# RMSNorm with relu: the scale and relu of eight rows in one vector instruction

## The chip, the cores and the metric

The kernel runs on one core of a Trainium2 chip. The metric is the device time of one execution in microseconds (us).

VectorE is called DVE in the profile, ScalarE is ACT, and SP is SyncE, which issues the large DMAs. "The period" below is the time from the start of one group of 8 rows on VectorE to the start of the next.

## The reference

```
x: 16 x 1024 x 512 float32, gamma: 512 float32, eps: 1e-5
rms    = sqrt(mean(x ** 2, over the last axis) + eps)
x_norm = x / rms * gamma
return maximum(x_norm, 0)
```

It reads 33.5 MB and writes 33.5 MB, and does little arithmetic on each element.

## The kernel before

The 16384 rows are cut into 8 chunks. A chunk has 16 rows on each of 128 partitions (4 MB) and lives in one of six slots. Everything is done in place in the slot. A chunk is computed in two groups of 8 rows (G = 8), so there are 16 groups in all.

```
K = 16
G = 8
nchunks = rows // K          # 8
nslots = 6
ngroups = K // G             # 2
# ... cut: pools, tiles, load() and store() of a whole chunk from SP ...

def compute(i):
    xt = slot[i % nslots]
    for g in range(ngroups):
        a, b = g * G, (g + 1) * G
        for j in range(a, b):
            nc.scalar.activation(out=junk, in_=xt[:, j, :], func=ACTF.Square,
                                 accum_out=ss[i][:, j:j + 1])
        nc.scalar.activation(out=rms[i][:, a:b], in_=ss[i][:, a:b],
                             func=ACTF.Sqrt, bias=eps_sb, scale=inv_d)
        nc.vector.tensor_mul(out=xt[:, a:b, :], in0=xt[:, a:b, :], in1=gammaG())
        nc.vector.reciprocal(out=rstd[i][:, a:b], in_=rms[i][:, a:b])
        for j in range(a, b):
            nc.vector.tensor_scalar(
                out=xt[:, j, :], in0=xt[:, j, :],
                scalar1=rstd[i][:, j:j + 1], scalar2=0.0,
                op0=ALU.mult, op1=ALU.max)

# ... cut: gamma copied to all partitions ...
for i in range(min(nslots, nchunks)):
    load(i)
for i in range(min(nslots, nchunks)):
    compute(i)
nxt = nslots
for i in range(nchunks):
    store(i)
    if i >= 1 and nxt < nchunks:
        load(nxt)
        compute(nxt)
        nxt += 1
```

`gammaG()` is gamma with a step of 0 over the eight rows: the same 512 values are read again for each row, with an innermost step of 1.

## Time and profile before

| | before |
|---|---|
| time, median | 164.25 us (163.35 to 164.48; 164.11 when the prediction was made) |
| span of the profile | 162.0 us |
| VectorE busy | 124.6 us, 77% |
| ScalarE busy | 98.5 us, 61% |
| large DMA queue, share of 16 engines | 96.9% |

These are lines of the page of the kernel before: busy time by engine, the 40 slices of VectorE and DMA (a digit is the busy share of a slice in tenths), the queue with the share of all 16 engines' time, the chain of waits that ended last (shares of the span by engine), and the two costliest vector groups (busy time in all, mean ns of one, then idle time before it).

```profile
DVE 124.6 (77%) x164; ACT 98.5 (61%) x274; POOL 0.2 (0%) x4
...
DVE  1001299999999999999999999999999999920000
...
DMA  6999899999999999998999999999999999999990
...
q1 hardware_dynamic: 2304, 67.11, 96.9%
...
DVE 74%; DMA 8%; ACT 3%; issue 2%; DVEq 0%
...
L78 DVE TENSOR_TENSOR slot<-slot,gamma_sb 128x4096 f32<-128x4096 f32 x16 | 70.7, 4418 | 4.2 <-ACT junk L74 4.2
L81 DVE TENSOR_SCALAR slot<-slot,rstd 128x512 f32<-128x512 f32 x128 | 52.1, 481 | 0.6
```

The averages (77%, 97%) leave open which engine sets the time, and the chain of waits (74% VectorE) seems to name VectorE. The slices say more. VectorE works without a gap from slice 6 to slice 35 and does nothing in the last four; from its end at 142.99 us to the end of the span it is idle for 19 us, while DMA is full until nearly the end.

The next lines are the timeline of VectorE for one period (start in us, duration in us, what). A mean of 481 ns for one tensor_scalar includes its overlap with the next (eight times 481 ns would be 3.85 us, and the eight below take 3.26 from the first start to the last end).

```profile
57.78 4.42 DVE L78 TENSOR_TENSOR slot<-slot,gamma_sb 128x4096 f32<-128x4096 f32 x1
62.12 0.19 DVE L79 RECIPROCAL rstd<-rms 128x8 f32<-128x8 f32 x1
62.35 3.26 DVE L81 TENSOR_SCALAR slot<-slot,rstd 128x512 f32<-128x512 f32 x8
65.52 4.42 DVE L78 TENSOR_TENSOR slot<-slot,gamma_sb 128x4096 f32<-128x4096 f32 x1
```

From start to start the multiply by gamma takes 4.34 us, the reciprocal 0.23 and the eight tensor_scalars 65.52 - 62.35 = 3.17. The period is 7.74 us. The multiply spends 1.06 ns on an element of a partition, the tensor_scalars 3.17 / 4096 = 0.77 ns with their fixed costs included.

The last store is issued when VectorE is done. Below are SP's own waits (waiter, what it waited for, us in total, times, longest); the second line is the wait for the last store. After them stand two stretches of the windows view: stretch and length, busy time of DVE, ACT and POOL, granted clock, DMA share, GB/s.

```profile
SPq L62 <- DVE slot L81: 94.5, 7, 20.7
...
SPq L133 <- DMA out_dram<-slot: 17.6, 1, 17.6
```

```profile
155.00:158.00 3.00, 0.00 (x0) 0.00 (x0) 0.00 (x0) 1.00 0.94 404
158.00:161.00 3.00, 0.00 (x0) 0.00 (x0) 0.00 (x0) 1.00 0.05 22
```

The last store of 4 MB needs 17.6 us after its issue, though 4 MB take 9.8 us at 430 GB/s, the rate of the windows view from 92 to 110 us. It stands in line behind earlier stores: DMA is near full up to 158 us, and the windows from 143 to 158 us (426 GB/s for 7 us, 446 for 5, 404 for 3) come to 6.4 MB, 2.2 MB more than the last store has.

### The profile page before, as it was taken

Reading aid. Unit: us, or ns where it says so; the run is one execution under the profiler, and the core shown is the slowest. Engines: PE = TensorE matmul, PEld = TensorE weight load, DVE = VectorE, ACT = ScalarE, POOL = GpSimd, SP = SyncE. Lnnn points to the kernel's source line nnn. Section 1 sums busy time; section 2 is a strip of 40 time slices with the busy share of each in tenths; the row PEclk is TensorE's granted clock in tenths of the full one; section 3 lists DMA queues with packets and bytes.
Section 4 is the critical chain, followed back from the end, with each engine's and each line's share of the span. In section 5 each row is a group of like instructions: output and inputs, shape, how many; then the busy total and the mean of one; then the engine's idle time right before and its main releaser. Section 6 shows DMA issues by size and latency. Waiting matters only on the chain.

```text
span 162.0 us, 554 instructions
## 1 busy us (share of the span) xinstructions
DVE 124.6 (77%) x164; ACT 98.5 (61%) x274; POOL 0.2 (0%) x4
## 2 busy tenths in 40 slices
DVE  1001299999999999999999999999999999920000
ACT  2107999999999999999999199901998000000000
POOL 0000000000000000000000000000000000000000
DMA  6999899999999999998999999999999999999990
GB/s 227 421 405 502 388 413 493 390 421 477 396 421 471 396 388 388 461 445 388 463 437 404 453 445 404 453 437 396 461 429 445 429 421 445 429 421 445 437 413 16
DMA packets 2315, 67.14 MB, mean 414 GB/s; under 512 B 260, under 2 KB 260, under 8 KB 264
## 3 DMA queue, kind: packets, MB, share of 16 engines
q1 hardware_dynamic: 2304, 67.11, 96.9%
q14 instruction: 3, 0.02, 0.0%
q10 hardware_dynamic: 8, 0.01, 0.0%
HBM read 33.56 MB, written 33.55 MB: 414 GB/s over the span
## 4 chain that ended last, share of the span: by engine, by line
DVE 74%; DMA 8%; ACT 3%; issue 2%; DVEq 0%
DVE slot L78 43%; DVE slot L81 30%; DMA slot<-in_x_dram 8%; ACT junk L74 3%; DVE rstd L79 1%; DVEq L133 0%
## 5 line engine op out<-in xcount | busy, mean ns | idle before, releaser
L74 ACT ACTIVATE junk<-slot 128x512 f32<-128x512 f32 x128 | 76.8, 600 | 23.0 <-DMA slot<-in_x_dram 19.5
L78 DVE TENSOR_TENSOR slot<-slot,gamma_sb 128x4096 f32<-128x4096 f32 x16 | 70.7, 4418 | 4.2 <-ACT junk L74 4.2
L81 DVE TENSOR_SCALAR slot<-slot,rstd 128x512 f32<-128x512 f32 x128 | 52.1, 481 | 0.6
L74 ACT ACTIVATION_READ_ACCUMULATOR junk<-slot 128x1 f32 x128 | 23.8, 186 | 0.0
L93 DVE LOAD_MASK_SELECT gamma_sb<-gseed x1 | 0.0, 14 | 12.8 <-DMA gseed<-in_gamma_dram 12.8
L76 ACT ACTIVATE rms<-ss,eps_sb 128x8 f32<-128x8 f32 x16 | 4.8, 301 | 0.5
L74 ACT ACT_TABLE_LOAD x1 | 1.3, 1283 | 3.2 <-issue 3.2
L79 DVE RECIPROCAL rstd<-rms 128x8 f32<-128x8 f32 x16 | 3.1, 194 | 0.0
L76 ACT ACT_TABLE_LOAD x1 | 1.3, 1283 | 0.0
L86 DVE MEMSET gseed<- 128x512 f32 x1 | 0.5, 485 | 0.9 <-PEq L119 0.9
L93 DVE STREAM_SHUFFLE gamma_sb<-gseed 128x512 f32<-128x512 f32 x1 | 0.7, 721 | 0.0
L119 POOL MEMSET const-bfloat16-1.0<- 128x1 bf16 x1 | 0.1, 101 | 0.0
L119 POOL MEMSET const-uint8-127<- 128x1 uint8 x1 | 0.1, 101 | 0.0
L119 POOL MEMSET const-float32-0.0<- 128x1 f32 x1 | 0.1, 99 | 0.2 <-issue 0.2
L119 POOL MEMSET const-float32-1.0<- 128x1 f32 x1 | 0.1, 98 | 0.0
L87 DVE MEMSET eps_sb<- 128x1 f32 x1 | 0.1, 59 | 0.0
## 6 DMA issues: line engine op xcount, KB each, us to landing
slot<-in_x_dram SPq DMA_DIRECT2D x8, 4096.0 KB, 30.6
out_dram<-slot SPq DMA_DIRECT2D x8, 4096.0 KB, 35.4
gseed<-in_gamma_dram ACTq DMA_DIRECT2D x4, 2.0 KB
```

The source lines that it names most:

```text
L74: nc.scalar.activation(out=junk, in_=xt[:, j, :], func=ACTF.Square, accum_out=ss[i][:, j:j + 1])
L76: nc.scalar.activation(out=rms[i][:, a:b], in_=ss[i][:, a:b], func=ACTF.Sqrt, bias=eps_sb, scale=inv_d)
L78: nc.vector.tensor_mul(out=xt[:, a:b, :], in0=xt[:, a:b, :], in1=gammaG())
L79: nc.vector.reciprocal(out=rstd[i][:, a:b], in_=rms[i][:, a:b])
L81: nc.vector.tensor_scalar(out=xt[:, j, :], in0=xt[:, j, :], scalar1=rstd[i][:, j:j + 1], scalar2=0.0, op0=ALU.mult, op1=ALU.max)
L86: nc.vector.memset(gseed, 0.0)
L87: nc.vector.memset(eps_sb, eps)
L93: nc.vector.stream_shuffle(gamma_sb, gseed, [0] * 32)
L119: nc = _bacc.Bacc("TRN2", target_bir_lowering=False, num_devices=1)
```

## The change

The intent is fewer vector instructions: eight small tensor_scalars per group become one scalar_tensor_tensor over all eight rows. It takes the max with 0 first and then multiplies by the row factor, which gives the same because the factor is positive. The row factor comes in as a second tensor, with a step of 0 along the row.

```diff
             nc.vector.reciprocal(out=rstd[i][:, a:b], in_=rms[i][:, a:b])
-            for j in range(a, b):
-                nc.vector.tensor_scalar(
-                    out=xt[:, j, :], in0=xt[:, j, :],
-                    scalar1=rstd[i][:, j:j + 1], scalar2=0.0,
-                    op0=ALU.mult, op1=ALU.max)
+            r = rstd[i][:, a:b]
+            rb = bass.AP(tensor=r.tensor, offset=r.offset,
+                         ap=[r.ap[0], r.ap[1], [0, d]])
+            nc.vector.scalar_tensor_tensor(
+                out=xt[:, a:b, :], in0=xt[:, a:b, :], scalar=0.0, in1=rb,
+                op0=ALU.max, op1=ALU.mult)
```

## The prediction

What is cut out of the recorded text is marked: figures and reasons for the rate of vector instructions, for their fixed cost and for a penalty on the step of 0 that no trace of this case showed. No cut figure is a term of the forecast's sum: 160.8 + 12.2 + 1.1 us comes to a span of 174, and with 2.1 us to a time of 176 us.

> # Prediction
>
> **What bounds the kernel now.** The page: span 162.0 us, VectorE (DVE) busy 77%, ScalarE 61%, DMA queue 96.9%. Two resources are nearly full. The chain that ended last runs 74% through VectorE; in the timeline its work is gapless from 19.09 us to 142.99 us, 16 groups at a period of 7.74 us, and the waits show none for it after 19.09. The last 4 MB store is issued at 143.0 and lands about 160.9, 17.6 us later, although 4 MB at 430 GB/s takes 9.8 us: the windows show DMA at 0.94 or more until 158 us, so that store stands behind a backlog of about 6 us. That backlog is all the slack that VectorE has.
>
> **What the change does.** Per group of 8 rows it removes 8 tensor_scalars (128x512) and adds one scalar_tensor_tensor over 128x4096, whose row factor is read with an innermost step of 0. 128 vector instructions become 16; order, loads, stores and ScalarE work stay.
>
> Removed: eight tensor_scalars take 3.26 us together, 0.407 us for 512 elements. [...] the multiply by gamma (two tensors, 128x4096) takes 4.42 us, cadence 4.33.
> Added: the new instruction has two tensor operands[...]; estimated from that multiply, 4.42 us, cadence 4.33. The saved fixed costs (7 per group[...]) are already inside the 3.26. So +1.1 us per group, period 8.8 to 8.9 us: +17 to +18 us of vector time (124.6 to about 142).
>
> **On the critical path.** VectorE ends at 19.1 + 16 x 8.85 = about 160.7 us instead of 143.0. Chunks are ready every 17.7 us while the remaining stores need 9.8 each, so the queue is empty when the last store is issued (some microseconds of DMA idle before the last two stores). It then takes about 12 us (the first load, unqueued, took 12.3) instead of 17.6: 5.5 us are hidden. Span 160.8 + 12.2 + 1.1 = 174; time is span + 2.1: **176 us**, +7%. Range 172 to 181. Faster by over 2%: 0.02; within 2%: 0.03; slower by over 2%: 0.95.
>
> **What would show each step.** scalar_tensor_tensor x16 at about 4.4 us (right)[...]. DVE busy about 142 us, gapless to about 160.7, no new wait. DMA share about 90%, low slices before the last store. SP's wait for the last store about 12 us. ScalarE busy unchanged.
>
> **What would make it wrong.** The read with innermost step 0 of a 4-byte operand. [...] I give any such penalty 10%. If the last store still finds a backlog, add 2 to 4 us; if it lands in 10.5 us, take 1.5 off.

## The result, and the profile after

| | before | after |
|---|---|---|
| time, median | 164.25 us | 175.74 us (175.59 to 175.76) |
| ratio to before | | 1.0708 (95% interval 1.0673 to 1.0743) |
| span | 162.0 us | 173.8 us |
| VectorE busy | 124.6 us | 143.3 us |
| vector instructions | 164 | 52 |
| VectorE ends at | 142.99 us | 161.64 us |
| wait for the last store | 17.6 us | 10.7 us |

A ratio is the mean time of one kernel's fast runs over that of the other's fast runs of the same rounds, so it is not quite the ratio of the medians.

The lines of the page after that answer to those of before:

```profile
DVE 143.3 (82%) x52; ACT 98.5 (57%) x274; POOL 0.2 (0%) x4
...
DVE  1001699999999999999999999999999999999100
...
DMA  6999899999999999989999999998989808930885
...
q1 hardware_dynamic: 2304, 67.11, 90.3%
...
DVE 49%; ACT 23%; issue 14%; DMA 7%
...
L78 DVE TENSOR_TENSOR slot<-slot,gamma_sb 128x4096 f32<-128x4096 f32 x16 | 70.7, 4419 | 4.1 <-ACT junk L74 4.1
L83 DVE SCALAR_TENSOR_TENSOR slot<-slot,rstd 128x4096 f32<-128x4096 f32 x16 | 70.8, 4425 | 0.5
```

The new instruction takes 4425 ns, the same as the multiply by gamma beside it. VectorE has a third of its former instructions and 18.7 us more of busy time. DMA has gaps (0, 3 and 0 tenths) in the last eight slices; before, only the very last slice was empty.

The chain of waits gives VectorE only 49% now, although VectorE does more. This share must not be read as relief. In the chain of this run, five of the last twelve new instructions are booked as "issue" in pieces of 4.31 us, and the first 54 us are traced back through ScalarE. The timeline shows VectorE without a wait from 19.03 us to its end. One period of it, after:

```profile
59.00 0.19 DVE L79 RECIPROCAL rstd<-rms 128x8 f32<-128x8 f32 x1
59.23 4.42 DVE L83 SCALAR_TENSOR_TENSOR slot<-slot,rstd 128x4096 f32<-128x4096 f32 x1
63.58 4.42 DVE L78 TENSOR_TENSOR slot<-slot,gamma_sb 128x4096 f32<-128x4096 f32 x1
67.91 0.20 DVE L79 RECIPROCAL rstd<-rms 128x8 f32<-128x8 f32 x1
68.14 4.42 DVE L83 SCALAR_TENSOR_TENSOR slot<-slot,rstd 128x4096 f32<-128x4096 f32 x1
```

From start to start the new instruction takes 4.35 us where the eight took 3.17, and the period is 68.14 - 59.23 = 8.91 us. The difference of 1.17 us comes 16 times, 18.7 us in all. The time rose by 11.5 us. The remaining 7 us are in the wait for the last store and in the windows at the end of the run:

```profile
SPq L62 <- DVE slot L83: 117.2, 7, 23.1
...
SPq L134 <- DMA out_dram<-slot: 10.7, 1, 10.7
```

```profile
155.00:158.00 3.00, 2.97 (x3) 0.00 (x0) 0.00 (x0) 1.00 0.00 0
158.00:161.00 3.00, 3.00 (x1) 0.00 (x0) 0.00 (x0) 1.00 0.00 0
161.00:165.00 4.00, 0.64 (x1) 0.00 (x0) 0.00 (x0) 1.00 0.75 319
```

DMA is idle from 155 to 161 us while VectorE works on the last group. The last store finds the queue empty and takes 10.7 us, 6.9 less than before.

### The profile page after: what moved, and what is told of

Its sections match the earlier page's. It is cut to its first block, busy times and chain, and to the rows that moved or that the text cites. A ratio compares the mean times of both kernels' runs of the same rounds, so it can differ in the third digit from the quotient of the medians.

```text
span 173.8 us, 415 instructions
## 1 busy us (share of the span) xinstructions
DVE 143.3 (82%) x52; ACT 98.5 (57%) x274; POOL 0.2 (0%) x4
## 3 DMA queue, kind: packets, MB, share of 16 engines
q1 hardware_dynamic: 2304, 67.11, 90.3%
## 4 chain that ended last, share of the span: by engine, by line
DVE 49%; ACT 23%; issue 14%; DMA 7%
DVE slot L78 30%; ACT junk L74 21%; DVE slot L83 18%; DMA slot<-in_x_dram 7%; ACT rms L76 1%; DVE rstd L79 1%; ACT L76 1%
## 5 line engine op out<-in xcount | busy, mean ns | idle before, releaser
L83 DVE SCALAR_TENSOR_TENSOR slot<-slot,rstd 128x4096 f32<-128x4096 f32 x16 | 70.8, 4425 | 0.5
```

The lines of the kernel that those rows point to most:

```text
L83: nc.vector.scalar_tensor_tensor(out=xt[:, a:b, :], in0=xt[:, a:b, :], scalar=0.0, in1=rb, op0=ALU.max, op1=ALU.mult)
```

## The experiments

There are two claims to test. The first is about the instruction: with the second tensor the rate is halved, and that costs more than the saved instructions give; the step of 0 has no part in it. The second is about the critical path: DMA is a floor, VectorE's work is free up to a certain end, and then each microsecond counts. The rivals were that long instructions are slow as such, that the step of 0 costs, and that VectorE's work counts in proportion. Twelve kernels ran. Each ratio is to the kernel before in the same rounds.

### e1_ts_one: one tensor_scalar over eight rows

```diff
-            for j in range(a, b):
-                nc.vector.tensor_scalar(
-                    out=xt[:, j, :], in0=xt[:, j, :],
-                    scalar1=rstd[i][:, j:j + 1], scalar2=0.0,
-                    op0=ALU.mult, op1=ALU.max)
+            nc.vector.tensor_scalar(
+                out=xt[:, a:b, :], in0=xt[:, a:b, :],
+                scalar1=rstd[i][:, a:a + 1], scalar2=0.0,
+                op0=ALU.mult, op1=ALU.max)
```

> Wrong result on purpose: the kernel before with ONE tensor_scalar over 128x4096 per group (row factor of the group's first row for all 8 rows). Only the count changes, from 8 to 1; the operation keeps its single tensor source. Theory (element rate decides, count only adds a fixed cost of about 0.13 us each):[...] about 2.27 us per instruction against 3.17 us for the eight; period about 6.8 us. Rival 1 ([...] the length is the culprit): about 4.4 us. For the time: theory of DMA as the floor says 164, same as before, although VectorE loses about 14 us of work; rival 2 (VectorE's work counts one for one, as its 74% of the chain suggests) says about 150.

The fixed cost of 0.13 us is measured at e12.

Measured: 163.98 us, ratio 0.9987 (0.9963 to 1.0011). The timeline of VectorE:

```profile
60.63 4.42 DVE L78 TENSOR_TENSOR slot<-slot,gamma_sb 128x4096 f32<-128x4096 f32 x1
64.96 0.19 DVE L79 RECIPROCAL rstd<-rms 128x8 f32<-128x8 f32 x1
65.19 2.35 DVE L80 TENSOR_SCALAR slot<-slot,rstd 128x4096 f32<-128x4096 f32 x1
67.46 4.42 DVE L78 TENSOR_TENSOR slot<-slot,gamma_sb 128x4096 f32<-128x4096 f32 x1
```

From start to start the tensor_scalar takes 67.46 - 65.19 = 2.27 us, as expected, and the multiply by gamma of the same size 64.96 - 60.63 = 4.33. So a long tensor_scalar keeps its rate (0.55 ns per element with the fixed cost, where the eight short ones have 0.77 and the multiply 1.06), and merging eight into one would save 0.90 us per group if the operation could stay what it is. It can't: one tensor_scalar has one factor per partition, and the eight rows need eight (the result of e1 was wrong by a relative error of 0.041). The time did not move although VectorE lost 14.3 us of busy time (110.3 against 124.6): the rival by which each vector microsecond counts is out. VectorE ended at 132.4 us, 10.6 us earlier than before (not 14.3, because it waited 3.7 us more for ScalarE), and SP waited for the last store 10.6 us longer, 28.2 in place of 17.6:

```profile
SPq L132 <- DMA out_dram<-slot: 28.2, 1, 28.2
```

### e2_stt_eight: the new operation, still eight times

```diff
+            for j in range(a, b):
+                r = rstd[i][:, j:j + 1]
+                rb = bass.AP(tensor=r.tensor, offset=r.offset,
+                             ap=[r.ap[0], [0, d]])
+                nc.vector.scalar_tensor_tensor(
+                    out=xt[:, j, :], in0=xt[:, j, :], scalar=0.0, in1=rb,
+                    op0=ALU.max, op1=ALU.mult)
```

(in place of the one instruction over eight rows)

> Right result: the changed kernel with its instruction cut into eight, scalar_tensor_tensor on 128x512 with the row factor read at step 0, so the kind of instruction changes and the count of 8 stays. Theory:[...] 0.60 to 0.66 us each, 4.8 to 5.3 us per group, period 9.4 to 9.9 us, VectorE ends at 170 to 177 us, time 184 to 191. So fewer instructions did help, by 0.5 to 1 us per group, and the rate lost more. Rival (the count is worth nothing when the rate is the same): 4.35 us per group and 176.

Measured: 183.61 us, ratio 1.1184 (1.1168 to 1.1201).

```profile
61.17 4.90 DVE L84 SCALAR_TENSOR_TENSOR slot<-slot,rstd 128x512 f32<-128x512 f32 x8
66.00 4.42 DVE L78 TENSOR_TENSOR slot<-slot,gamma_sb 128x4096 f32<-128x4096 f32 x1
```

VectorE ended at 169.3 us. End and time lie just under the expected ranges (170 to 177 and 184 to 191), because the instructions came out at the low edge of theirs, 0.604 us each. From start to start the eight take 4.83 us, so the count is worth something (0.48 us per group against 4.35 for one), and the rival that gives it no worth is out. Four corners are now known, in us per group from start to start:

| | eight of 128x512 | one of 128x4096 |
|---|---|---|
| tensor_scalar, one tensor source | 3.17 (before) | 2.27 (e1) |
| scalar_tensor_tensor, two tensor sources | 4.83 (e2) | 4.35 (after) |

Going right gains 0.9 or 0.5 us. Going down loses 1.7 or 2.1. The change goes right and down at once. The slope between the sizes gives the rate: (2.27 - 0.396) / 3584 = 0.523 ns per element for one source, (4.35 - 0.604) / 3584 = 1.045 ns for two. From one row of the table to the other, the operation and the number of tensor sources change together, and no run separates them. That the number of tensors decides is supported by the multiply by gamma: it is another operation with two tensors, and its 4.34 us for the same size is the same rate.

### e3_stt_rows and e9_step0_no_recip: is the step of 0 at fault?

The first puts gamma's rows (innermost step 1) in the place of the row factor:

```diff
# ... cut: rb, which is no longer used, is not made ...
-                out=xt[:, a:b, :], in0=xt[:, a:b, :], scalar=0.0, in1=rb,
+                out=xt[:, a:b, :], in0=xt[:, a:b, :], scalar=0.0, in1=gammaG(),
```

> Wrong result on purpose: the changed kernel with gamma (read again for each row, innermost step 1) in place of the row factor at innermost step 0 as the second tensor of scalar_tensor_tensor. Theory (the step of 0 costs nothing[...]): 4.42 us mean, 175.7 in time, same as the changed kernel within 0.5 us. Rival (reading one word over and over costs or saves something): another duration than 4.42 us.

Measured: 173.92 us, ratio 1.0596 (1.0578 to 1.0614). The instruction took 4425 ns, as in the changed kernel, so at the level of the instruction the step of 0 costs nothing:

```profile
L81 DVE SCALAR_TENSOR_TENSOR slot<-slot,gamma_sb 128x4096 f32<-128x4096 f32 x16 | 70.8, 4425 | 0.0
```

But the time was 1.8 us below the changed kernel, outside the half microsecond that the theory allowed. The edit had changed a second thing: the instruction no longer needed the reciprocal just ahead of it. A second run keeps the step of 0 and takes only that dependence away:

```diff
-            r = rstd[i][:, a:b]
+            r = rms[i][:, a:b]
```

> Wrong result on purpose: the changed kernel, its second tensor still read at step 0, but from the root mean square (ScalarE's result, long ready) in place of its reciprocal. The run with gamma's rows came out 1.8 us under the changed kernel although its scalar_tensor_tensor took the same 4425 ns; there the instruction started 0.11 us after the reciprocal's start, in the changed kernel 0.23 us. Theory (that difference is the hand-over from the reciprocal, whose result the instruction no longer needs, 16 x 0.11 us = 1.8): 0.11 us and about 173.9 here too, with the step of 0 kept. Rival (reading rows in place of a step of 0 is what saved it): 175.7.

Measured: 173.81 us, ratio 1.0583 (1.0561 to 1.0606), on the same chip as a control (below) with 175.79.

```profile
58.68 0.20 DVE L79 RECIPROCAL rstd<-rms 128x8 f32<-128x8 f32 x1
58.79 4.42 DVE L83 SCALAR_TENSOR_TENSOR slot<-slot,rms 128x4096 f32<-128x4096 f32 x1
63.14 4.42 DVE L78 TENSOR_TENSOR slot<-slot,gamma_sb 128x4096 f32<-128x4096 f32 x1
```

The instruction now starts 0.11 us after the reciprocal's start and before its end at 58.88 us; with the dependence it was 0.23 us, which is after the reciprocal's end (59.19 us there, where the instruction started at 59.23). Sixteen times 0.12 us is 1.9 us, and the time fell by 2.0. The step of 0 is cleared, in duration and in time. What e3 found is the price of waiting for a small result of the instruction just before; it is paid before and after the change alike (0.23 us from start to start in both).

### e10_after_again: control

The changed kernel without an edit.

> The changed kernel again, as the control on the same chip: 175.6 to 175.9.

Measured: 175.79 us, ratio 1.0701 (1.0679 to 1.0724), on another chip than the first time. The result repeats.

### e12_ts_imm: what the fixed part of the eight tensor_scalars is

The fixed part of one instruction is its time less 512 elements at the slope above: for a tensor_scalar 0.396 - 0.268 = 0.13 us, for a scalar_tensor_tensor 0.604 - 0.535 = 0.07 us. One difference between them is that the tensor_scalar reads its factor from memory as a scalar, one value per partition.

```diff
-                    scalar1=rstd[i][:, j:j + 1], scalar2=0.0,
+                    scalar1=1.0, scalar2=0.0,
```

> Wrong result on purpose: the kernel before with the constant 1.0 in place of the row factor in its eight tensor_scalars, so nothing is read per partition as a scalar. In the runs so far the fixed part was 0.128 us for a tensor_scalar with a scalar read from memory[...], 0.069 us for scalar_tensor_tensor with a constant[...]. Theory (reading the scalar from memory costs 0.05 to 0.07 us per instruction, and the change saved that too): 0.33 to 0.35 us each, 2.65 to 2.8 us for the eight in place of 3.17. Rival[...]: 3.17 us. Time same as before, 164, in both, as DMA is the floor.

Two fixed parts with the measured slopes are 2.21 - 4096 x 0.523 ns = 0.07 us for the tensor_scalar with constants and 0.68 - 0.535 = 0.14 us for the scalar_tensor_tensor with a scalar read from memory (both in e4, below). The rival was that the operation with 0.523 ns per element has the larger fixed part as such.

Measured: 164.18 us, ratio 1.0024 (0.9996 to 1.0052).

```profile
59.83 2.77 DVE L81 TENSOR_SCALAR slot<-slot 128x512 f32<-128x512 f32 x8
62.52 4.42 DVE L78 TENSOR_TENSOR slot<-slot,gamma_sb 128x4096 f32<-128x4096 f32 x1
```

The eight take 62.52 - 59.83 = 2.69 us, 0.336 each: reading the scalar from memory costs 0.06 us per instruction. Without it the fixed part of the tensor_scalar is 0.336 - 0.268 = 0.07 us, that of the scalar_tensor_tensor. The change per group, 4.35 - 3.17 = +1.18 us, can then be divided: +2.14 for the halved rate (4096 elements at 1.045 in place of 0.523 ns), about -0.48 for the fixed part paid once in place of eight times (seven times 0.069), and -0.48 for eight scalars no longer read from memory. As the terms come from the same durations, this divides the difference and is not a further check on it.

### e4_fused_gamma: another split of the same work

```diff
-            nc.vector.tensor_mul(out=xt[:, a:b, :], in0=xt[:, a:b, :], in1=gammaG())
             nc.vector.reciprocal(out=rstd[i][:, a:b], in_=rms[i][:, a:b])
             for j in range(a, b):
-                nc.vector.tensor_scalar(
-                    out=xt[:, j, :], in0=xt[:, j, :],
-                    scalar1=rstd[i][:, j:j + 1], scalar2=0.0,
-                    op0=ALU.mult, op1=ALU.max)
+                nc.vector.scalar_tensor_tensor(
+                    out=xt[:, j, :], in0=xt[:, j, :],
+                    scalar=rstd[i][:, j:j + 1], in1=gamma_sb[:],
+                    op0=ALU.mult, op1=ALU.mult)
+            nc.vector.tensor_scalar(
+                out=xt[:, a:b, :], in0=xt[:, a:b, :], scalar1=0.0, scalar2=None,
+                op0=ALU.max)
```

> Right result: another split of the same work. Per row one scalar_tensor_tensor (x times row factor) times gamma, in place of the multiply by gamma and the factor, then one single-source max with 0 over 128x4096. Per group 8 x 0.60 to 0.66 plus 2.27 plus 0.2 for the reciprocal: 7.3 to 7.8 us against 7.74 before; VectorE ends between 136 and 144 us. With DMA as the floor the time is 163.5 to 165, same as before, even if VectorE got faster. Rival (VectorE's work counts one for one): 157 to 165 in proportion to the period.

Measured: 164.11 us, ratio 0.9993 (0.9974 to 1.0013), result correct. The expectation for VectorE was missed: it ended at 146.75 us, not at 136 to 144. The period was 7.86 us, because each scalar_tensor_tensor took 0.68 us instead of 0.60 to 0.66. It too reads a scalar from memory and took 0.07 us more than the 0.604 of e2, which reads none; no run tests that cause for this operation alone. One period of VectorE and its last instruction:

```profile
60.39 5.39 DVE L80 SCALAR_TENSOR_TENSOR slot<-slot,rstd,gamma_sb 128x512 f32<-128x512 f32 x8
65.81 2.29 DVE L84 TENSOR_SCALAR slot<-slot 128x4096 f32<-128x4096 f32 x1
68.02 0.20 DVE L78 RECIPROCAL rstd<-rms 128x8 f32<-128x8 f32 x1
...
144.46 2.29 DVE L84 TENSOR_SCALAR slot<-slot 128x4096 f32<-128x4096 f32 x1
```

The single tensor_scalar with constants takes 68.02 - 65.81 = 2.21 us, 0.06 less than the one of e1 that reads a scalar: as much as the price found in e12. For the question it served even better than planned: VectorE ended 3.8 us later than in the kernel before, and the time did not move.

### e11_quarter, e5_first_half, e6_second_half: how much delay is free, and where

The change in some chunks only:

```diff
+            if i < 2:          # e11; i < 4 in e5; i >= 4 in e6
+                # the one scalar_tensor_tensor of the change
+            else:
+                # the eight tensor_scalars of before
```

> Right result: the change only in chunks 0 and 1. VectorE gets 4 x 1.18 = 4.7 us more and ends at about 147.7 us. Theory of slack: the last store lands at 160.9 before and takes 10.7 us unhindered, so VectorE may end up to about 150 us at no cost: time 164.2, same as before. Rival (each group costs its share of the 11.5 us): 167.0.

> Right result: the change only in chunks 0 to 3, the old eight tensor_scalars in chunks 4 to 7. VectorE gets half of the added work, 8 x 1.18 = 9.4 us, and ends at about 152.4 us. Theory (the first 6 us or so of delay are hidden behind the backlog of stores, and after that each microsecond counts): last store issued at 152.4 with the DMA queue just empty, lands 10.7 us later, time about 166.3, so +2 us. Rival (half the change costs half of its 11.5 us): 170.

> Right result: the change only in chunks 4 to 7. Theory: VectorE never waits, so where the delay is put does not matter, only the end of its work does: 152.4 us and 166.3 in time as in the other half. Rival (only late chunks reach the end, early ones are absorbed by waiting stores): this one carries nearly the whole 11.5 us, about 174, and the first half almost none, 164.5.

Measured: e11 163.94 us, ratio 0.9978 (0.9958 to 0.9998); e5 166.4 us, ratio 1.0134 (1.0115 to 1.0152); e6 166.56 us, ratio 1.0143 (1.0125 to 1.0161). A quarter of the change costs nothing, half of it 2 us, all of it 11.5 us. Where the half is put makes no difference. Both rivals, the proportional one and the one by which only late chunks count, are out. (The small gain of e11 has no cause that was tested; it is within 0.3% and was not taken for a faster version.) SP's waits for the last store in e11 and e5, in this order:

```profile
SPq L141 <- DMA out_dram<-slot: 13.2, 1, 13.2
```

```profile
SPq L141 <- DMA out_dram<-slot: 10.8, 1, 10.8
```

In e11 part of the line of stores is still there; in e5 it is gone and the wait has reached the 10.7 to 10.8 us of an unhindered store.

### e7_after_split and e8_before_split: the last stores in halves

The same edit was made in the changed kernel (e7) and in the kernel before (e8):

```diff
     def store(i):
-        nc.sync.dma_start(out=ov[i], in_=slot[i % nslots])
+        step = G if i >= nchunks - 2 else K
+        for h in range(0, K, step):
+            nc.sync.dma_start(out=ov[i][:, h:h + step, :],
+                              in_=slot[i % nslots][:, h:h + step, :])
```

> Right result: the changed kernel, with the stores of the last two chunks in two halves of 2 MB, each issued when its group is done. Theory (DMA stands idle for 6 to 7 us before the last store, and what is exposed at the end is the transfer of the last store): the last half is issued at 161.6 as before, but takes about 5.8 us in place of 10.7, so time 170.5 to 171. VectorE's work unchanged. Rival (the end is a fixed latency or another wait): 175 to 176.

> Right result: the kernel before with the same split of the last two stores. Theory (its last store stands behind a backlog, the queue has no idle time to be filled): DMA still ends at about 158 to 160 us, time 164 within 0.8. Rival (the last store's 4 MB is exposed here as well): 159 to 160.

Measured: e7 170.67 us, ratio 1.0395 (1.0378 to 1.0412); e8 164.37 us, ratio 1.0001 (0.9982 to 1.0019). The wait for the last store in e7, then one window of e7 and the same window of e8:

```profile
SPq L137 <- DMA out_dram<-slot: 5.8, 1, 5.8
```

```profile
155.00:158.00 3.00, 2.97 (x3) 0.00 (x0) 0.00 (x0) 1.00 1.01 431
```

```profile
155.00:158.00 3.00, 0.00 (x0) 0.00 (x0) 0.00 (x0) 1.00 1.02 437
```

VectorE ends at the same 161.6 us, and the part of the last store behind it is halved: 5 us come back. DMA is at 1.01 from 155 to 158 us, where the changed kernel had 0.00. In the kernel before, the same edit does nothing, since its queue had no gap to fill (0.94 in this window before, 1.02 in e8).

### All runs on one line

| run | VectorE ends at, us | time, us | time less end |
|---|---|---|---|
| e1 | 132.4 | 163.98 | 31.6 |
| e12 | 134.0 | 164.18 | 30.2 |
| before | 143.0 | 164.25 | 21.3 |
| e8 (half stores at the end) | 143.0 | 164.37 | 21.4 |
| e4 | 146.8 | 164.11 | 17.3 |
| e11 | 147.8 | 163.94 | 16.1 |
| e5 | 152.2 | 166.40 | 14.2 |
| e6 | 152.6 | 166.56 | 14.0 |
| e3 | 159.8 | 173.92 | 14.1 |
| e9 | 160.0 | 173.81 | 13.8 |
| after | 161.6 | 175.74 | 14.1 |
| e10 | 161.9 | 175.79 | 13.9 |
| e2 | 169.3 | 183.61 | 14.3 |
| e7 (half store at the end) | 161.6 | 170.67 | 9.1 |

The end is that of the last vector instruction in the profile. The runs with whole stores follow one rule: the time is the larger of 164 us and the end of VectorE plus 14 us. The two meet at about 150 us. The kernel before stands 7 us left of that corner, and the change moves it 11.6 us to the right of it.

That DMA is what holds the 164 us is read from its 97% and from four kernels (e1, e12, e4, e11) in which VectorE ended between 10.6 us earlier and 4.8 us later without effect on the time; no run changed the amount or the shape of all transfers. No version was found that beats both kernels. All correct ones with VectorE left of the corner take 164 us; in the kernel before, the DMA queue is then at 96.9% of its engines' time. Whether the transfers themselves could be made shorter was not tried.

## Why the prediction was right

The prediction was 176.0 us, the result 175.74 us. Point by point:

- **The rate.** It set the new instruction, with its two tensors, at the time of the multiply by gamma (4.33 us from start to start) and the removed ones at their own 3.26 us. The new instruction took 4.35. The rates are 0.523 ns per element for the tensor_scalar and 1.045 for the scalar_tensor_tensor (e1, e2 and both kernels). Why the rate is halved was not shown: no run looks into that.
- **The step of 0** was named as the main risk and given 10%. It costs nothing: 4425 ns with it and without it, and the time follows the dependence alone (e3, e9).
- **The size per group** was a little off. "+1.1 us per group, period 8.8 to 8.9" was 1.17 to 1.18 us and 8.91. The term mis-sized is "eight tensor_scalars take 3.26 us together": this is a busy time with the tail of the last one, and it was set against a start-to-start time of 4.33. Start to start they take 3.17. So VectorE ended at 161.64 us, not 160.7, and was busy for 143.3 us, not 142.
- **Fixed costs** of the removed instructions were already inside their measured time, as it said. Measured, they were 0.13 us each, of which 0.06 is the scalar read from memory (e12).
- **The last store** was put at 12 us from the first load's 12.3, and took 10.7; the prediction had named this case ("if it lands in 10.5 us, take 1.5 off"). Here it was too slow by 1.3 us, and the two errors of about 1 us cancelled. That the total came within 0.3 us is luck; the mechanism and each term's size to about 1 us are not.
- **The slack** was put at "about 6 us". Taken from the corner it is 7 us. That the rest of the delay is paid in full, after the backlog is used up, is what e5, e6 and e11 show.
- **DMA share about 90%** was 90.3%, with empty slices before the last store. ScalarE was unchanged at 98.5 us, and VectorE had no new wait.

## What to carry to other kernels

Fewer instructions are worth their fixed costs (here 0.07 us each, and 0.06 more for a scalar read from memory), and that has to be weighed against the rate: an operation with a broadcast second tensor, at 1.045 ns per element, took the place of one at 0.523, 2.1 us lost on 4096 elements for less than 1 us saved. Before a change of this kind, read start-to-start times, not means or busy times, and divide by the elements. And find out by how much the engine's end may move before it is felt: with DMA near full (here 97%), a line of waiting stores can hide a slower engine for some microseconds (here about 7: VectorE ended 4.8 us later in e11 at no cost in time), and a faster one was worth nothing (10.6 us earlier in e1, the same time).
